# One store of a cross-covariance attention kernel, half of it sent in parts of 92, 4 and 32 partitions

## The chip, the core and the metric

The kernel runs on one core of one Trainium2 chip. The metric is device time in microseconds (us): the median of the runs of the program. Beside it there is one profiled execution with its trace. The work of the core is done by TensorE (PE, with its weight loads shown as PEld), VectorE (DVE), ScalarE (ACT) and GpSimd (POOL); SyncE (SP) issues nearly all transfers between the chip's memory (HBM) and the on-chip buffers, and sixteen DMA engines carry them out.

## The reference, cut to what matters

```python
batch, heads, seq, dim = 8, 12, 512, 64          # Q, K, V: float32
Q_norm = Q / (np.linalg.norm(Q, axis=-2, keepdims=True) + 1e-10)
K_norm = K / (np.linalg.norm(K, axis=-2, keepdims=True) + 1e-10)
attn = np.einsum('bhnd,bhne->bhde', Q_norm, K_norm)
attn = softmax(attn, axis=-1)                    # written out with max, exp and sum
out  = np.einsum('bhnd,bhde->bhne', V, attn)
```

There are 96 heads. For each, a 64x64 matrix is made of Q and K, normalised, put through a softmax, and applied to V. Three inputs of 12.58 MB are read and one output of 12.58 MB is written.

## The kernel before, in words

**Tiling.** Four heads make a unit `u` (24 of them), two units a step `s` (`S` = 12), two steps a pair `w` (6). Q and K of a unit are loaded (`load_qk`, lines 182 to 186), cast to bf16 (`cast_qk`, L206), multiplied into Gram matrices (`grams`, L226), from which the norms and the logits come; V is loaded (`load_v`), cast, transposed (`vtrans`) and copied to `vt`. The output matmuls (`outs`, L312) write PSUM, and `ocopy` (L165 on ACT, L167 on DVE) brings the results into a tile `so[s, i]` of 128 partitions.

**Stores.** `so[s, i]` with `i` 0 or 1 holds half of a step: 128 partitions, for each of two units `r` a contiguous run of 2 KB (`J * D` = 512 floats). So a store moves 256 rows of 2 KB, 512 KB in all. `store(s, i)` issues it as one DMA on SP (L200); the very last tile (`s` = 11, `i` = 1) goes in two DMAs of 256 KB with rows of 1 KB. There are 25 store DMAs. Every DMA of the kernel spans 128 partitions.

**Order.** All work is put into one list by a planner (`Order.run`) that simulates the engines and a DMA queue of eight; each transfer has a due rank. It puts 5 of the stores between the loads, and the last 20 DMAs on SP are all stores, in the order of `s` and `i`. On SP a DMA waits for its data and, by one of eight semaphores used in turn, for the complete landing of the DMA issued eight places earlier on SP. The end of the kernel (L492) waits for all of them.

Of the kernel before, what the change touches and what calls it, by code (L numbers as in the profile page):

```python
# [102 lines left out]
def kernel(  # L103
# [7 lines left out]
    nc = tc.nc  # L111
# [3 lines left out]
    S = U // 2  # L115
# [3 lines left out]
    ONE = 3  # L119
    HELD, UNTIL = ("lk", 1, 1), ("cq", 0, 1)  # L120
    BOTH = S - 8

# [36 lines left out]
    qk32, v32, vb, qkb, gram, scr, kq, n2, r8, kqs, rq, lg, ex, ab, vps, vt, po, so = ({} for _ in range(18))  # L161
# [35 lines left out]
    def store(s, i, k=None):  # L197
        rows = slice(None) if k is None else slice(k * (J // 2), (k + 1) * (J // 2))
        o = Of[s // 2, s % 2, i].rearrange("p r (j d) -> p r j d", d=D)
        nc.sync.dma_start(out=o[:, :, rows], in_=so[s, i][:, :, rows])  # L200

    def cast_qk(u, x):
# [138 lines left out]
    for i in range(NB["ab"]):  # L341
        a = const.tile([128, HU, 2 * D], BF16, name=f"ab{i}")
# [17 lines left out]
    def piece(key, engines, after, behind, rank, fn, *args):  # L360
        if key[0] in ("cv", "vc", "oc", "kq", "sc"):
            plan.add(key, engines, after, behind, rank, lambda eng: fn(eng, *args))
        else:
            plan.add(key, engines, after, behind, rank, lambda eng: fn(*args))

    def back(kind, i, n, *rest):
        return (kind, i - n, *rest) if i - n >= 0 else None
# [17 lines left out]
    for u in range(U):  # L385
        s, r = divmod(u, 2)
# [21 lines left out]
    for w in range(W):  # L408
        both = 2 * w >= BOTH
        for r in range(2):  # L410
# [24 lines left out]
    for s in range(S):  # L435
        for x in range(4):
            i, k = divmod(x, 2)
            n = 4 * s + x - 2
            wait = [("oc", n // 4, n % 4)] if n >= 0 else []
            order = [("ou", s, x - 1) if x else back("ou", s, 1, 3)]  # L440
            piece(("ou", s, x), {"PE": 0.5}, [("vc", s // 2, *t) for t in turns(s // 2) if t[0] // 2 == k] + [("nm", s)] + wait, order, R["ou"] + 0.01 * s, outs, s, x)
            n = 2 * s + i - NB["so"]
            free = [("st", n // 2, n % 2)] if k == 0 and n >= 0 else []
            order = [("oc", s, x - 1) if x else back("oc", s, 1, 3)]
            piece(("oc", s, x), {"ACT": 0.6, "DVE": (0.68, BIAS["oc"])} if s >= BOTH else {"ACT": 0.6}, [("ou", s, x)] + free, order, R["oc"] + 0.01 * s, ocopy, s, x)
        for i in range(2):
            order = [("st", s, 0) if i else back("st", s, 1, 1)]
            if (s, i) == (S - 1, 1):

                piece(("sh", s, i), {"DMA": 0.67}, [("oc", s, 2)], order, v_at(2 * s + i) + ST_LAG, store, s, i, 0)  # L450
                piece(("st", s, i), {"DMA": 0.67}, [("oc", s, 3)], [("sh", s, i)], v_at(2 * s + i) + ST_LAG, store, s, i, 1)
            else:
                piece(("st", s, i), {"DMA": X}, [("oc", s, 2 * i), ("oc", s, 2 * i + 1)], order, v_at(2 * s + i) + ST_LAG, store, s, i)
# [43 lines left out]
```

## Time and profile before

| what | us |
|---|---|
| median of 3 runs | 128.83 (128.76 to 129.06) |
| profiled execution, its own time | 129.06 |
| its span, first to last instruction | 127.3 |
| last compute instruction ends (ACT, L165) | 115.34 |
| last store DMA issued on SP | 117.29 |
| DVE busy / PE busy / ACT busy | 93.0 / 79.4 / 72.5 |
| mean rate of the DMA engines | 398 GB/s |

The page shows one execution. Its second part cuts the span into 40 slices of 3.18 us; the row DMA is the mean busy share of the 16 DMA engines. Part 3 lists the DMA queues: q1 is SP's, q10 ACT's, and the two of kind "instruction" fetch program code. A DMA that is split over all engines is finished when each of the sixteen has finished its share; the trace marks each of these sixteen landings, without the number of the engine.

### The profile page before, as it was taken

The page shows a single profiled execution, that of the slowest core. Times are in us where ns is not written, and L with a number is a line of the kernel's source. Part 1 is how long each engine was busy: PE and PEld are TensorE (multiplying, and loading weights), DVE is VectorE, ACT ScalarE, POOL GpSimd, SP SyncE. Part 2 cuts the span into 40 slices and gives each one's busy share as a digit, 9 for nine tenths or more (in the row PEclk, how much of TensorE's full clock was granted, in tenths as well). Part 3 has the DMA queues.
Part 4 walks back from the last instruction along what each step waited for, and adds up shares of the span by engine and source line. Part 5 has one row for each costly group of instructions (what it writes and reads, how often), then busy time and mean ns, then how long its engine had stood idle before and what let it go on. Part 6 is the DMA issues. An engine that isn't in the chain of part 4 may idle for free.

```text
span 127.3 us, 4884 instructions
## 1 busy us (share of the span) xinstructions
PE 79.4 (62%) x2128; PEld 64.0 (50%) x2128; DVE 93.0 (73%) x141; ACT 72.5 (57%) x220; POOL 36.3 (28%) x40
## 2 busy tenths in 40 slices
PE   0065384894844589859873996698975869580000
PEld 0055372773633568648661885486764748460000
DVE  3263649959999899998986798999999799820000
ACT  4000441569777068785792789384949969972000
POOL 4005306300915913033064203213453361200000
PEclk9999999999997556995999589655699995955555
DMA  3999999999999999999999999999999999999992
GB/s 107 404 434 409 430 409 418 415 440 402 425 429 416 407 418 424 407 416 422 430 415 409 417 424 417 417 420 424 406 413 407 406 401 406 400 407 407 408 352 98
DMA packets 15605, 50.64 MB, mean 398 GB/s; under 512 B 1120, under 2 KB 1632, under 8 KB 14176
## 3 DMA queue, kind: packets, MB, share of 16 engines
q1 hardware_dynamic: 15296, 49.29, 96.2%
q10 hardware_dynamic: 288, 1.05, 2.1%
q8 instruction: 16, 0.26, 0.7%
q14 instruction: 5, 0.04, 0.1%
HBM read 37.75 MB, written 12.58 MB: 396 GB/s over the span
## 4 chain that ended last, share of the span: by engine, by line
DVE 31%; DMA 20%; PE 18%; ACT 14%; issue 4%; SPq 2%; POOL 1%; DVEq 0%; POOLq 0%; ACTq 0%
DMA qk<-in_K_dram 14%; PE gram L226 12%; DVE qkb L206 11%; DVE scr L233 6%; DMA qk<-in_Q_dram 5%; DVE ab L284 5%; ACT so L165 4%; ACT vt L165 4%; ACT ex L275 4%; PE vps L295 3%; DVE vt L167 3%; DVE n L245 3%; PE po L312 2%; ACT kq L165 1%; SPq L184 1%
## 5 line engine op out<-in xcount | busy, mean ns | idle before, releaser
L226 PE MATMUL gram<-qkb 32*128 32x128 bf16 (+1 forms) x1504 | 35.6, 255 | 21.9 <-DVE qkb L206 8.8
L206 DVE CAST qkb<-qk 128x1024 bf16<-128x1024 f32 x48 | 37.3, 801 | 8.5 <-DMA qk<-in_Q_dram 7.0
L226 PEld LDWEIGHTS <-qkb 32*128 32x128 bf16 (+1 forms) x1504 | 29.8, 114 | 26.8 <-DVE qkb L206 11.6
L169 POOL TENSOR_SCALAR vb<-v 128x1024 bf16<-128x1024 f32 x19 | 21.2, 1126 | 45.1 <-DMA v<-in_V_dram 45.0
L165 ACT COPY so<-po 128x512 f32<-128x512 f32 x45 | 25.0, 593 | 6.6 <-PE po L312 6.4
L165 ACT COPY vt<-vps 128x1024 bf16<-128x1024 bf16 (+1 forms) x18 | 17.8, 987 | 15.9 <-PE vps L295 15.9
L312 PE MATMUL po<-ab,vt 128*64 128x128 bf16 x384 | 21.1, 259 | 6.0 <-issue 2.4
L295 PE MATMUL vps<-identb,vb 128*128 128x128 bf16 x192 | 19.3, 255 | 5.1 <-POOL vb L169 3.1
L256 POOL TENSOR_TENSOR kqs<-kq,r 64x512 f32<-64x512 f32 x12 | 13.7, 1143 | 26.9 <-ACT r L252 13.7
L312 PEld LDWEIGHTS <-vt 128*64 128x64 bf16 x384 | 15.3, 131 | 10.3 <-issue 5.4
L233 DVE SCALAR_TENSOR_TENSOR scr<-gram,eye 64x512 f32<-64x512 f32 x24 | 16.5, 688 | 4.7 <-PE gram L226 4.4
L295 PEld LDWEIGHTS <-vb 128*128 128x128 bf16 x192 | 14.1, 113 | 9.0 <-POOL vb L169 4.5
L275 ACT ACTIVATE ex<-lg,rq 128x64 f32<-128x64 f32 x48 | 14.5, 321 | 2.8 <-PE lg L269 2.8
L165 ACT COPY kq<-gram 64x512 f32<-64x512 f32 x12 | 7.0, 580 | 13.6 <-DVE scr L233 13.4
L284 DVE TENSOR_TENSOR ab<-ex,rinv 64x256 bf16<-64x256 f32 x24 | 13.2, 548 | 0.6
L275 ACT ACTIVATION_READ_ACCUMULATOR ex<-lg,rq 128x1 f32 x48 | 10.2, 213 | 0.0
L167 DVE CAST vb<-v 128x1024 bf16<-128x1024 f32 x5 | 7.4, 1483 | 1.3 <-DMA v<-in_V_dram 1.2
L269 PE MATMUL lg<-eye,kqs 64*128 64x64 f32 x48 | 6.9, 274 | 2.3 <-POOL kqs L256 1.8
L245 DVE TENSOR_REDUCE n<-scr 128x8 f32<-128x512 f32 x12 | 8.2, 679 | 0.1
L167 DVE COPY vt<-vps 128x1024 bf16<-128x1024 bf16 (+1 forms) x8 | 7.9, 1019 | 0.1
L269 PEld LDWEIGHTS lg<-eye,kqs 64*128 64x128 f32 x48 | 4.8, 168 | 4.3 <-POOL kqs L256 2.5
L281 DVE RECIPROCAL rinv<-esum 128x4 f32<-128x4 f32 x12 | 2.1, 172 | 2.6 <-ACT ex L275 2.5
(17 smaller groups left out, 16.0 us busy)
## 6 DMA issues: line engine op xcount, KB each, us to landing
out_dram<-so SPq DMA_DIRECT2D x23, 512.0 KB, 10.2
v<-in_V_dram SPq DMA_DIRECT2D x11, 1024.0 KB, 17.2
qk<-in_Q_dram SPq DMA_DIRECT2D x8, 1024.0 KB, 17.5
qk<-in_K_dram SPq DMA_DIRECT2D x8, 1024.0 KB, 18.5
qk<-in_Q_dram SPq DMA_DIRECT2D x8, 512.0 KB, 12.2
qk<-in_K_dram SPq DMA_DIRECT2D x6, 512.0 KB, 12.4
qk<-in_K_dram ACTq DMA_DIRECT2D x2, 512.0 KB, 6.3
v<-in_V_dram SPq DMA_DIRECT2D x2, 512.0 KB, 10.6
```

Of the source, the lines that this page charges most:

```text
L165: nc.scalar.copy(o, i)
L167: nc.vector.tensor_copy(o, i)
L169: nc.gpsimd.tensor_scalar(out=o, in0=i, scalar1=1.0, scalar2=0.0, op0=ALU.mult, op1=ALU.add)
L206: nc.vector.tensor_copy(qkb[u][:, :, x * D:(x + 1) * D], qk32[s][:, x, r])
L226: nc.tensor.matmul(gram[s][:, h, r, 0], x, x, start=(t == 0), stop=(t == (T if u < WIDE else J) - 1))
L233: nc.vector.scalar_tensor_tensor(out=scr[s][half], in0=gram[s][half, :, :, 0, half].rearrange("p h r d -> p (h r) d"), scalar=1e-20, in1=e ...
L245: nc.vector.tensor_reduce(out=n2[s], in_=scr[s], axis=mybir.AxisListType.X, op=ALU.add)
L256: (nc.vector if eng == "DVE" else nc.gpsimd).tensor_tensor(out=kqs[s][HI], in0=kq[s][HI], in1=r8[s][HI, :, None].to_broadcast([D, 2 * HU, ...
L275: nc.scalar.activation(e[:, h, :], lg[s][:, h, :], AF.Exp, scale=rq[s][:, h:h + 1], accum_out=z[:, h:h + 1])
L284: nc.vector.tensor_tensor(out=a[half, :, half], in0=e[half], in1=ri[half, :, None].to_broadcast([D, HU, D]), op=ALU.mult,)
L295: nc.tensor.transpose(ps[:, c, n, :], vb[w][:, J * c + j].rearrange("p r d -> p (r d)"), identb)
L312: nc.tensor.matmul(po[s, x][e * D:(e + 1) * D, j].rearrange("p r d -> p (r d)"), v, ab[s][:, h, :])
```

## The change

The store of step `S - 3` = 9, `i` = 1 (the sixth DMA from the end of SP's list of 20) is sent as four DMAs in place of one. Its half `r` = 1 goes as one DMA of 128 partitions. Its half `r` = 0 goes as three: partitions 0 to 91, 92 to 95 and 96 to 127. As the change is described, the first two of these run on the four lowest DMA engines alone, and the third on all sixteen.

```diff
+    FEW = (S - 3, 1)
...
     def store(s, i, k=None):
         rows = slice(None) if k is None else slice(k * (J // 2), (k + 1) * (J // 2))
         o = Of[s // 2, s % 2, i].rearrange("p r (j d) -> p r j d", d=D)
+        if (s, i) == FEW:
+            for a, b in ((0, 92), (92, 96), (96, 128)):
+                nc.sync.dma_start(out=o[a:b, 0], in_=so[s, i][a:b, 0])
+            nc.sync.dma_start(out=o[:, 1], in_=so[s, i][:, 1])
+            return
         nc.sync.dma_start(out=o[:, :, rows], in_=so[s, i][:, :, rows])
```

The order of all other instructions on every engine stays as it was.

## The prediction

> **What bounds the kernel now.** I began with the page's slices and queues.
>
> ```profile
> span 127.3 us, 4884 instructions
> DMA  3999999999999999999999999999999999999992
> ## 3 DMA queue, kind: packets, MB, share of 16 engines
> q1 hardware_dynamic: 15296, 49.29, 96.2%
> q10 hardware_dynamic: 288, 1.05, 2.1%
> q8 instruction: 16, 0.26, 0.7%
> q14 instruction: 5, 0.04, 0.1%
> ```
>
> From the second slice to the last but one the DMA engines are full. No compute engine is: DVE is busy for 73% of the span. So the kernel is bound by bytes, and the chain of waits, which follows only compute instructions, ends 12 us before the span does. The end is made by the stores. I looked at SP's last rows next: the timeline's last row, then the time to landing of the stores from 93 us on, then SP's waits from 85 us on.
>
> ```profile
> 117.29 0.71 SPq L200 DMA_DIRECT2D out_dram<-so  x1
> ```
>
> ```profile
> DMA to landing us min/median/max: 9.0/10.2/10.2
> ```
>
> ```profile
> SPq L200 <- DMA out_dram<-so: 8.8, 14, 1.0
> SPq L492 <- DMA out_dram<-so: 8.2, 3, 6.9
> ```
>
> The last store is issued at 117.29 and lands 9.0 us later, at 126.29; SP's closing wait (L492) is for it, and the span ends 0.97 us after. The profiled execution took 129.06 us, 1.8 more than its span and 0.23 above the median of the runs, 128.83. I make the sum against the landing at 126.29 and take 0.23 off at the end.
>
> The question is whether all sixteen engines finish together. Narrow windows answer it (second last column: busy share of 16 engines; last: GB/s).
>
> ```profile
> 121.00:122.00 1.00, 0.00 (x0) 0.00 (x0) 0.00 (x0) 0.00 (x0) 0.00 (x0) 0.50 1.05 402
> 122.50:123.00 0.50, 0.00 (x0) 0.00 (x0) 0.00 (x0) 0.00 (x0) 0.00 (x0) 0.50 0.96 358
> 123.00:123.50 0.50, 0.00 (x0) 0.00 (x0) 0.00 (x0) 0.00 (x0) 0.00 (x0) 0.50 0.80 299
> 123.50:124.00 0.50, 0.00 (x0) 0.00 (x0) 0.00 (x0) 0.00 (x0) 0.00 (x0) 0.50 0.68 260
> 124.00:124.50 0.50, 0.00 (x0) 0.00 (x0) 0.00 (x0) 0.00 (x0) 0.00 (x0) 0.50 0.55 205
> 125.00:125.50 0.50, 0.00 (x0) 0.00 (x0) 0.00 (x0) 0.00 (x0) 0.00 (x0) 0.50 0.55 195
> 125.50:126.00 0.50, 0.00 (x0) 0.00 (x0) 0.00 (x0) 0.00 (x0) 0.00 (x0) 0.50 0.22 74
> ```
>
> They don't. Full is 1.05; from 124 to 125.5 the share is 0.55, so some eight engines work on while eight are done. The sixteen landing marks of the last store in the trace say the same: 123.10, 123.13, 123.20, 123.50, 123.68, 123.96, 124.37, 124.60, and then eight from 125.87 to 126.29. Every transfer of this kernel gives each engine the same bytes, so the lag comes from elsewhere. Queue q8 has 16 packets of 16 KB; the trace puts each at 0.88 to 0.96 us, on one engine alone. Followed from landing to landing, all engines step evenly, except that after each q8 packet one engine falls back by about 1.4 us; eight engines do so, twice each. The 8 KB packets of q14 (0.31 us) fall on the other eight, with steps of 0.5 to 0.8. So the program's own code is fetched unevenly over the DMA engines, and that sets who ends last.
>
> **The change, part by part.**
>
> *Price of a row.* At 402 GB/s an engine moves 25.1 GB/s, 0.082 us for a row of 2 KB; stores land 1.28 us apart with 16 rows per engine, 0.080 each. I take 0.080.
>
> *Rows moved.* The half `r` = 0 gave each engine 8 rows. By the change's own account it now gives the four lowest 92/4 + 4/4 + 32/16 = 26 rows and the other twelve 2. So +18 rows = +1.44 us for four engines, -6 rows = -0.48 us for twelve.
>
> *Three more DMAs.* Each adds one completion mark per engine (a 4-byte packet, 9 ns in the trace). The four get three more, the twelve one more: +0.03 and +0.01 us. On SP each issue took 0.37 to 0.85 us in this stretch, which lies within the 1.28 us between two stores.
>
> [...]
>
> *SP's queue.* Each SP DMA waits for the one eight places earlier. Three more DMAs push the five stores behind them three places down, so each is issued some 3 x 1.28 = 3.84 us later: the last at about 120 us. The early engines need its rows only from about 123.8 and the late ones from 125, so 3.8 us and more hide it (before, the first packet moved 1.0 us after the first issue). The last DMA now also waits for the part of 92 partitions. On four early engines that is done at about 118.5 (their landing of the DMA before, 116.6 to 117.0, plus 23 rows = 1.84), which is earlier. Cost nothing; with the cover gone it would be up to 3.84.
>
> *Where the rows go.* All hangs on which engines are the lowest four, and the trace does not number them. If they are among the eight that carry no q8 packet, they end at 123.10 to 124.60 plus 1.47, that is 124.57 to 126.07, and the eight late ones at 126.29 - 0.47 = 125.82. Unless the slowest of that early half (124.60) is one of the four, or the next (124.37, which then ends at 125.84, as good as level), the late eight set the end at 125.82: a gain of 0.47. With the slowest, the end is 126.07: a gain of 0.22. I take 0.47, since the four marks nearest together, 123.10 to 123.50, are the likeliest to be neighbours, and keep 0.22 for the range.
>
> *Reading from other partitions.* No row shows a store that gives one engine 23 rows in place of 8. [...] I take nothing, by the nearest rows: packets of 2, 4 and 8 KB took 84, 159 and 309 ns on loads and stores alike, whatever the other fifteen engines were reading or writing at the time. [...]
>
> **Sum.** Profiled: the last landing moves from 126.29 to 125.82, and with what lies around the span unchanged 129.06 - 0.47 = 128.59. The median of the runs lies 0.23 lower: 128.36. I say 128.4.
>
> **The rivals.**
>
> *The four lowest fetch code (slower).* If even one of the four is among the eight late engines, that one ends at 125.87 to 126.29 plus 1.47, so 127.3 to 127.8, and nothing takes work off it. Price +1.05 to +1.47: about 130.2. The point from which it decides is a landing before of 126.29 - 1.47 = 124.82 or later; between 124.60 and 125.87 there is no engine, so it is one or the other. For it: only 8 of 16 engines are early, and all four must be. When the very first load begins, the sixteen first packets come in four groups of four by their durations; in the two groups that I could follow, two engines later fetch code and two do not. Were these groups neighbours by number, the lowest four would hold two late ones. Against: engines that serve one fetch queue in a fixed rotation of eight look like one half of sixteen, not like picks among them, and then it is a matter of which half.
>
> *The early four fill up (no change).* One of them is the engine of 124.60, or their rows run somewhat slower than 0.080: with 18 rows at 0.09 to 0.10 the slowest early engine ends at 126.2 to 126.4. Time 128.6 to 128.95.
>
> *The split isn't what it says.* If 92 partitions also run on all sixteen engines, nothing is moved; three completion marks cost 0.03: 128.85. Against it: nothing in the trace, as all its DMAs span 128 partitions. [...]
>
> **How the numbers follow.** About 0.2% (0.26 us) is what a measurement of this kernel can tell from no change. The early engines take the rows, gain 0.47: 0.42. One of the four was late: 0.38. Filled up: 0.16, and no split: 0.04, together the 0.20 for no change. The likeliest case alone has 128.2 to 128.6 (a row at 0.082 and the lowest run at one end, half a gain at the other). The two signs lie so close in chance that the range must hold the slow case too: up to 130.4, its 130.3 with the spread of the runs.
>
> **What would show it.** Right: the busy share falls from 1.05 later than 122.5 and from there to nothing within some 2 us; the last store's eight last marks come 0.47 earlier; four marks in the middle come 1.47 later; SP issues its last store near 120. Wrong: a share of 0.25 (four engines) or less for 1.5 us at the end, with twelve marks earlier and at least one beyond 127.3; or a last store that is issued after 121 and lands only then; or rows of 2 KB that take over 84 ns while the part of 92 is under way.

## The result, and the profile after

The changed kernel takes 128.61 us (median of 20 runs, 128.46 to 128.80) against 128.93 for the kernel before on the same chip (20 runs, 128.76 to 129.10). The ratio is 0.9976, with a 95% interval of 0.997 to 0.9983: a gain of 0.31 us, between 0.22 and 0.39. The profiled execution took 128.80 us, 0.26 less than that of before. In every profiled execution of this document the time is that of the last landing mark plus 2.62 to 2.79 us: the last mark decides.

The page of the changed kernel, slices and queues: the bytes and the code packets are as before, q1 has 24 packets more.

```profile
span 127.0 us, 4887 instructions
DMA  4999999999999999999999999999999999999993
q1 hardware_dynamic: 15320, 49.29, 96.4%
q8 instruction: 16, 0.26, 0.7%
```

Of the 24, one completion mark more on each of twelve engines and three more on each of four would be 12 + 12: that is the count if the parts of 92 and 4 partitions run on four engines alone. The timeline of SP at the end shows the parts (L204, L205) and the last five stores behind them:

```profile
110.63 2.80 SPq L204 DMA_DIRECT2D out_dram<-so  x3
114.40 0.37 SPq L205 DMA_DIRECT2D out_dram<-so  x1
115.75 4.76 SPq L207 DMA_DIRECT2D out_dram<-so  x5
```

The last issue starts at 120.05, 2.76 later than before, and no engine waited for it: the last store's marks follow those of the store before it by some 0.68 us, as they did before the change. Narrow windows of the changed kernel (second last column: share of the 16 DMA engines):

```profile
122.50:123.00 0.50, 0.00 (x0) 0.00 (x0) 0.00 (x0) 0.00 (x0) 0.00 (x0) 0.50 0.87 336
123.00:123.50 0.50, 0.00 (x0) 0.00 (x0) 0.00 (x0) 0.00 (x0) 0.00 (x0) 0.50 0.87 334
123.50:124.00 0.50, 0.00 (x0) 0.00 (x0) 0.00 (x0) 0.00 (x0) 0.00 (x0) 0.50 0.78 281
124.00:124.50 0.50, 0.00 (x0) 0.00 (x0) 0.00 (x0) 0.00 (x0) 0.00 (x0) 0.50 0.81 287
124.50:125.00 0.50, 0.00 (x0) 0.00 (x0) 0.00 (x0) 0.00 (x0) 0.00 (x0) 0.50 0.65 229
125.00:125.50 0.50, 0.00 (x0) 0.00 (x0) 0.00 (x0) 0.00 (x0) 0.00 (x0) 0.50 0.12 41
125.50:126.00 0.50, 0.00 (x0) 0.00 (x0) 0.00 (x0) 0.00 (x0) 0.00 (x0) 0.50 0.03 10
```

Where before 0.55 of the engines were at work from 124 to 125.5, now some twelve are (0.81) until 124.5, and the fall comes half a microsecond earlier. One engine is left over: 0.03 after 125.5. The landing marks of the last store say which: four early ones (122.48, 122.69, 123.03, 124.00), eleven between 124.81 and 125.54, and a single one at 126.05. The marks of the part of 92 partitions belong to four engines: 118.70, 118.95, 119.30, 119.94. Each of these four ends 6.11 or 6.12 us later (124.81, 125.07, 125.41, 126.05), so the slowest of them stays the last to the end.

The two profiles alone don't show the gain. In the one of the changed kernel the store before the parts already stood 0.27 us earlier (last mark 119.52 against 119.79), and from there to the end it took 6.53 us against 6.50: nothing was won in this execution. The gain of 0.31 us is that of the 20 runs; the repeat below has a profile in which the change wins its full share.

### The profile page after: what moved, and what is told of

It is laid out like the page before. It is cut to its first block, busy times and chain, and to the rows that moved or that the text cites. A ratio compares the mean times of both kernels' runs of the same rounds, so it can differ in the third digit from the quotient of the medians.

```text
span 127.0 us, 4887 instructions
## 1 busy us (share of the span) xinstructions
PE 77.7 (61%) x2128; PEld 62.9 (50%) x2128; DVE 92.8 (73%) x141; ACT 72.5 (57%) x220; POOL 36.6 (29%) x40
## 3 DMA queue, kind: packets, MB, share of 16 engines
q1 hardware_dynamic: 15320, 49.29, 96.4%
## 4 chain that ended last, share of the span: by engine, by line
DVE 39%; DMA 21%; PE 13%; ACT 11%; issue 4%; POOL 2%; DVEq 0%; SPq 0%; POOLq 0%; ACTq 0%
DMA qk<-in_Q_dram 21%; DVE qkb L213 15%; PE gram L233 9%; DVE scr L240 7%; DVE ab L291 6%; ACT vt L166 4%; DVE vb L168 4%; ACT ex L282 3%; ACT so L166 3%; PE vps L302 3%; DVE n L252 2%; DVE vt L168 2%; DVE so L168 2%; PE po L319 1%; ACT kq L166 1%
## 5 line engine op out<-in xcount | busy, mean ns | idle before, releaser
L213 DVE CAST qkb<-qk 128x1024 bf16<-128x1024 f32 x48 | 36.4, 780 | 8.5 <-DMA qk<-in_Q_dram 6.9
L302 PE MATMUL vps<-identb,vb 128*128 128x128 bf16 x192 | 20.2, 262 | 5.8 <-POOL vb L170 3.7
L319 PE MATMUL po<-ab,vt 128*64 128x128 bf16 x384 | 19.3, 242 | 5.2 <-issue 2.7
L302 PEld LDWEIGHTS <-vb 128*128 128x128 bf16 x192 | 14.7, 117 | 10.0 <-POOL vb L170 5.1
L319 PEld LDWEIGHTS <-vt 128*64 128x64 bf16 x384 | 13.8, 121 | 9.2 <-issue 4.6
L291 DVE TENSOR_TENSOR ab<-ex,rinv 64x256 bf16<-64x256 f32 x24 | 13.9, 579 | 0.6
L282 ACT ACTIVATION_READ_ACCUMULATOR ex<-lg,rq 128x1 f32 x48 | 10.2, 213 | 0.0
L276 PE MATMUL lg<-eye,kqs 64*128 64x64 f32 x48 | 6.4, 259 | 2.6 <-issue 1.5
## 6 DMA issues: line engine op xcount, KB each, us to landing
out_dram<-so SPq DMA_DIRECT2D x22, 512.0 KB, 10.2
```

Of the source, the lines that this page charges most:

```text
L213: nc.vector.tensor_copy(qkb[u][:, :, x * D:(x + 1) * D], qk32[s][:, x, r])
L276: nc.tensor.transpose(l[:, h, :], kqs[s][HI, 2 * h:2 * h + 2].rearrange("p r d -> p (r d)"), eye2[HI])
L282: nc.scalar.activation(e[:, h, :], lg[s][:, h, :], AF.Exp, scale=rq[s][:, h:h + 1], accum_out=z[:, h:h + 1])
L291: nc.vector.tensor_tensor(out=a[half, :, half], in0=e[half], in1=ri[half, :, None].to_broadcast([D, HU, D]), op=ALU.mult,)
L302: nc.tensor.transpose(ps[:, c, n, :], vb[w][:, J * c + j].rearrange("p r d -> p (r d)"), identb)
L319: nc.tensor.matmul(po[s, x][e * D:(e + 1) * D, j].rearrange("p r d -> p (r d)"), v, ab[s][:, h, :])
```

## The experiments

Each time stands against runs of the kernel before on the same chip; those runs had medians of 128.93 to 129.02. "Rows" are runs of 2 KB; the line changed is the `for` of the change, if nothing else is shown.

**Splitting without shifting.**

```diff
-            for a, b in ((0, 92), (92, 96), (96, 128)):
+            for a, b in ((0, 96), (96, 112), (112, 128)):
```

> The same store in the same number of DMAs, but with parts of 96, 16 and 16 partitions, which give every engine 8 rows as before: split without shift. Theory (rows moved off the late engines make the gain): no change against before, within 0.2%, near 128.9; the sixteen marks of the last store spread over 3.2 us as before. Rival (the gain comes from the splitting itself, from smaller parts or from the later issue of the stores behind): as fast as the changed kernel, 0.3 us under before.

Measured: 129.03 against 128.99, ratio 1.0002 (0.9993 to 1.0011). The last store's marks run from 123.04 to 126.33, as wide as before. From the last mark of the store before the parts to the end it is 6.50 us, as before. So three DMAs more, and the later issue behind them, cost nothing and bring nothing that can be told: the gain is in the shift.

**The whole half on four engines.**

```diff
-            for a, b in ((0, 92), (92, 96), (96, 128)):
+            for a, b in ((0, 124), (124, 128)):
```

> Parts of 124 and 4 partitions: the whole half on the four lowest engines, 32 rows each in place of 8 (+24), the other twelve -8. Theory (the changed kernel now ends on the slowest of the four lowest, at 126.05): six rows more on it, 126.05 + 0.48 = 126.5 for the last mark, the late eight at 125.4; 0.48 slower than the changed kernel, 0.1 to 0.2 us slower than before. Rival (the late eight still set the end in most runs): 0.16 faster than the changed kernel, 0.5 faster than before.

Measured: 128.96, ratio 1.0003 (0.9994 to 1.0011): the gain is gone, though the slow-down of 0.1 to 0.2 that I expected is not resolved. The trace's last mark is at 126.52, as reckoned, and the one before it at 125.85. Its windows show a long thin tail that the changed kernel has not:

```profile
125.00:125.50 0.50, 0.00 (x0) 0.00 (x0) 0.00 (x0) 0.00 (x0) 0.00 (x0) 0.50 0.16 55
125.50:126.00 0.50, 0.00 (x0) 0.00 (x0) 0.00 (x0) 0.00 (x0) 0.00 (x0) 0.50 0.07 25
126.00:126.50 0.50, 0.00 (x0) 0.00 (x0) 0.00 (x0) 0.00 (x0) 0.00 (x0) 0.50 0.02 8
```

One engine (0.02 to 0.07 of sixteen) sets the end: more rows for the four is worse from here on.

**Numbering the engines.**

```diff
-            for a, b in ((0, 92), (92, 96), (96, 128)):
+            for a, b in ((0, 96), (96, 108), (108, 116), (116, 120),
+                         (120, 123), (123, 125), (125, 126), (126, 128)):
```

> One look to number the engines: the half leaves in parts of 96, 12, 8, 4, 3, 2, 1 and 2 partitions, so that the part of n partitions marks only its engines. Theory (the eight engines that fetch no PE code are the lowest eight): the part of 8 has eight early marks and none from the late eight, the part of 12 has four late ones. Rival (they are picked from among the sixteen): the part of 8 has late marks too, beyond the four lowest. Either way the parts of 4, 3, 2 and 1 tell which of the four lowest is the one that ends last. Its time is not read: eight small DMAs in a row take most of SP's eight places.

The part of 96 has sixteen marks, eight from 116.97 to 118.92 and eight from 119.65 to 120.11. The part of 12 has seven early and five late ones, that of 8 six early (117.38 to 119.29) and two late (120.11, 120.21), that of 4 only early ones: 117.70, 118.02, 118.39, 118.98. So none of engines 0 to 3 is late, two of 4 to 7, three of 8 to 11 and three of 12 to 15: the rival is right that they are picked. (The trace gives no numbers. That a part on n engines uses 0 to n - 1 is my assumption, in line with the account of the change; no run shows it, and every number of an engine in this document rests on it.) The slowest of the four lowest is in the parts of 3, 2 and 1 (119.17, 119.34, 119.50), so it is engine 0, 1.5 us behind the earliest engine, which by that assumption no part can leave out. The part of 96 has sixteen marks, and each smaller part as many as it has partitions: with the sixteen of the other half 64 in place of the 16 of one store, and q1 has 48 packets more than before (15344 against 15296). In the changed kernel the part of 92 has four marks. These counts leave out one mark more that the parts on fewer than sixteen engines have; in the changed kernel it comes 0.46 us after the issue of the part of 92 and 0.43 us after that of the part of 4 (111.09 and 112.25), long before their data. The one run took 130.18 us.

**Less code to fetch.** From the kernel before:

```diff
-        for t in range(T if u < WIDE else J):
+        for t in range(4):
...
-                nc.tensor.matmul(gram[s][:, h, r, 0], x, x, start=(t == 0), stop=(t == (T if u < WIDE else J) - 1))
+                nc.tensor.matmul(gram[s][:, h, r, 0], x, x, start=(t == 0), stop=(t == 3))
```

> The kernel before with Gram matrices over 4 of the 16 (or 8) rows, so that TensorE has about 2250 instructions fewer and its code takes 7 packets of 16 KB in place of 16; the transfers are the same, the Gram sums are partial. Theory (PE's code packets make the lag of the late engines): seven engines late by 1.4 us once, none twice; the last store's marks spread over about 1.5 us in place of 3.2 and the time falls by some 1.4 us to 127.5. Rival (those engines are late for another reason, or the end hangs on compute): spread of 3.2 us and no change beyond 0.3 us.

Measured: 127.63 against 128.99, ratio 0.99 (0.9885 to 0.9914), 1.3 us faster, and the repeat (below) 127.54, ratio 0.9894. The page of the repeat shows the same transfers, half the code packets (8; I had reckoned 7) and still full DMA engines:

```profile
span 126.0 us, 2644 instructions
DMA  4999999999999999999999999999999999999993
q1 hardware_dynamic: 15296, 49.29, 97.1%
q8 instruction: 8, 0.13, 0.4%
```

The marks of the last store run from 123.03 to 125.21 in the first trace and from 123.26 to 125.05 in the repeat: a spread of 2.2 and 1.8 us (expected 1.5) in place of 3.2. The earliest mark is about where it was (123.10 before), so it is the late engines that gain, and less computing as such has not made all transfers faster. The 0.13 MB of code left out, spread over all engines at 402 GB/s, would be an estimated 0.33 us.

**The change where half of the lag is gone.** The edit of the last experiment and the change together, beside the former alone.

> The change on top of the shortened Gram matrices (4 of 16 rows, partial sums), where half of TensorE's code packets are gone. Theory (the change pays only because code fetching holds eight engines back): without most of that lag the four lowest end 1.47 later than in the shortened kernel, at about 125.7 to 126.0 against its last mark of 125.21, so it is 0.4 to 0.8 us slower than the shortened kernel. Rival (the parts pay by themselves): 0.3 us faster than the shortened kernel.

> The shortened Gram matrices without the change once more, beside e9 on the same chip: 1.3 us (1.1 to 1.5) faster than before by every theory.

Measured: 128.53 with the change (ratio to before 0.9969, 0.9958 to 0.998), 127.54 without it (0.9894, 0.988 to 0.9908): the same edit that gains 0.3 us now costs 1.0, a little more than expected (0.8 between the two profiles). The windows of the shortened kernel with the change:

```profile
124.00:124.50 0.50, 0.00 (x0) 0.00 (x0) 0.00 (x0) 0.00 (x0) 0.00 (x0) 0.50 0.26 92
124.50:125.00 0.50, 0.00 (x0) 0.00 (x0) 0.00 (x0) 0.00 (x0) 0.00 (x0) 0.50 0.16 55
125.00:125.50 0.50, 0.00 (x0) 0.00 (x0) 0.00 (x0) 0.00 (x0) 0.00 (x0) 0.50 0.09 31
```

A share of 0.26 is four engines, 0.09 a little over one. Four marks stand alone, 124.77, 125.04, 125.47 and 125.84; the other twelve are done by 124.39. Without the change the DMA engines of this kernel are done earlier:

```profile
124.00:124.50 0.50, 0.00 (x0) 0.00 (x0) 0.00 (x0) 0.00 (x0) 0.00 (x0) 0.50 0.53 186
124.50:125.00 0.50, 0.00 (x0) 0.00 (x0) 0.00 (x0) 0.00 (x0) 0.00 (x0) 0.50 0.07 23
```

This settles the cause: the change pays only because of the lag that code fetching makes.

**The changed kernel once more, with fewer rows, and earlier.** The repeat has no edit. Then

```diff
-            for a, b in ((0, 92), (92, 96), (96, 128)):
+            for a, b in ((0, 76), (76, 80), (80, 128)):
```

and, with the parts of the change,

```diff
-    FEW = (S - 3, 1)
+    FEW = (S - 6, 1)
```

> The changed kernel once more, beside the next three on the same chip: 0.3 us (0.2 to 0.4) faster than before by every theory; its last mark belongs to the slowest of the four lowest engines, some 0.5 us after the late eight.

> Parts of 76, 4 and 48 partitions: the four lowest get 23 rows in place of 26 (+15 over before), the others 3 in place of 2 (-5). Theory (the slowest of the four, engine 0, ends the changed kernel 0.5 us after the late eight): engine 0 ends at 126.05 - 0.24 = 125.81, the late eight at 125.54 + 0.08 = 125.62, so 0.24 faster than the changed kernel and 0.5 faster than before. Rival (in most runs the late eight end last, as the prediction had it): 0.08 slower than the changed kernel, 0.24 faster than before.

> The change's parts of 92, 4 and 32 put on a store three steps earlier (S - 6). Theory (rows are moved between engines that are always full, and SP's queue hides the later issue wherever it is): same as the changed kernel within 0.1 us. Rival (the gain needs the shift at the very end, or the queue's shorter backlog costs something there): no gain over before, or a loss.

Measured, against 129.02: the repeat 128.71 (ratio 0.9973, 0.9963 to 0.9982), fewer rows 128.52 (0.9963, 0.9951 to 0.9976), earlier 128.53 (0.9966, 0.9953 to 0.9978). The rival of "earlier" falls: the place of the shift doesn't matter by more than can be told. Fewer rows gain 0.48 against 0.35 for the repeat; the intervals overlap, so that they beat the change is likely and not shown. The traces tell why the step is smaller than 0.24: in the repeat the slowest mark of the four lowest came 0.21 earlier than in the first profile (119.91 against 120.12 after the part of 4), and the last five marks of its last store lie together from 125.66 to 125.93. From the last mark of the store before the parts to the end the repeat took 6.02 us (119.90 to 125.93) against 6.53 in the first profile and 6.50 before, and the kernel with fewer rows took 6.10 (119.80 to 125.91). Engine 0's lag changes from one execution to the next, for a reason that no run shows; so does which group ends last, and my "some 0.5 us after the late eight" held in one profile of two.

**The eight lowest engines.**

```diff
-            for a, b in ((0, 92), (92, 96), (96, 128)):
-                nc.sync.dma_start(out=o[a:b, 0], in_=so[s, i][a:b, 0])
-            nc.sync.dma_start(out=o[:, 1], in_=so[s, i][:, 1])
+            for a, b in ((0, 96), (96, 104), (104, 112), (112, 120), (120, 128)):
+                nc.sync.dma_start(out=o[a:b], in_=so[s, i][a:b])
```

> The same store as a part of 96 partitions and four of 8 partitions, both halves in each: the eight lowest engines get 20 rows in place of 16 (+4), the other eight 12 (-4). By the stairs two of the late engines are among engines 4 to 7. Theory: these two end 4 rows later, 126.29 + 0.32 + 0.03 = 126.6, so 0.35 us slower than before: what the change would have cost had its engines been late ones, at a quarter of its rows. Rival (the numbering read from the stairs is wrong, and the lowest eight are all early): 0.3 faster than before.

Measured: 128.98, ratio 0.9996 (0.9987 to 1.0005), no change. Both expectations missed. My error can be read in the stairs: the two late engines among 4 to 7 are not the latest of the eight. Going back from their marks at 120.11 and 120.21 by two parts of one row each, they stand at about 119.7 and 119.8 in the part of 96, where the latest is at 120.11. With 0.3 to 0.4 in hand, 0.35 more brings them level with the old end, while the other late ones gain. The trace of this run agrees. Its parts of 8 again have six early marks and two late ones, and these two were the earliest of the late eight in the store before (119.19 and 119.29, the latest 119.82), with 0.5 to 0.6 in hand. After the last part of 8 they stand at 120.98 and 121.08, behind the other late ones (at most 120.78 after the part of 96), and they are the last from then on, to 126.15 against 126.29 before.

**Both small gains together.** Parts of 76, 4 and 48 on the store of `S - 6`.

> Parts of 76, 4 and 48 partitions on the store three steps earlier: the two experiments that came out ahead of the changed kernel together. Theory: the late eight set the end with 5 rows less, 126.29 - 0.40 + 0.01 = 125.9, so 0.4 faster than before and at most 0.1 from either of the two alone. Rival (position and size add up): 0.6 faster than before.

Measured: 128.49 against 128.93, ratio 0.9965 (0.9952 to 0.9977), 0.45 faster; last mark 125.76. That is nearest to the theory's 0.4, but the interval is a gain of 0.30 to 0.62 us, and the rival's 0.6 lies just inside it: that position and size don't add up is likely and not shown.

## Why the prediction was right, point by point

**The range** says little: 128.2 to 130.4 held the slow rival and no change as well. The point was 128.4, and the likeliest case alone had 128.2 to 128.6, at whose edge 128.61 lies. What counts is what follows.

**The direction and the mechanism** held. DMA engines that lag by their code packets set the end (halving the packets: -1.3 us), the shift takes rows off them, and the split itself is free (ratio 1.0002).

**The price of a row** held. In the changed kernel the four engines land the part of 92 partitions 1.85 us after the store before (116.85 to 118.70, 117.10 to 118.95): 23 rows at 0.080. The late eight need 6.02 us from the last mark of the store before the parts to their own last mark (119.52 to 125.54), against 6.50 before (119.79 to 126.29): -0.48, where the sum had -0.47. The four themselves need 7.96 us (118.09 to 126.05 for the slowest), against 6.51 of an early engine before (116.59 to 123.10): +1.45, where the sum had +1.47. Reading 92 partitions by four engines cost nothing, as those 23 rows at 0.080 show, and I was right to take nothing.

**The three extra DMAs and SP's queue** were free, as taken: splitting alone gave a ratio of 1.0002. In the profile of before a store took 10.2 us from issue to landing while one landed each 1.28 us, so some eight were under way at once. Of SP's waits from 85 us on, the closing one shows where its time went:

```profile
SPq L499 <- DMA out_dram<-so: 5.4, 3, 3.9
```

The closing wait is 3.9 us at the longest in place of 6.9, since the last store is issued later, at 120.05 as reckoned, though 2.76 and not 3.84 later than before. The last store waited for the part of 92 partitions, whose slowest engine landed at 119.94, only 0.42 after the store before the parts (119.52) and not a full 1.28. So that part did set the last issue. The prediction had put it at about 118.5 on all four engines; it was 118.70 to 119.94. The prediction also took 123.8 as the time from which the early engines need the last store's rows. That overlooked the four early engines that get fewer rows: the first of them had finished the store before at 121.80. The issue at 120.05 was early enough for it too.

**What was mis-sized is the end of the slowest of the four.** The forecast took 0.47, arguing that the four marks nearest together (123.10 to 123.50) are the likeliest neighbours. They are not: before their part the four lowest stood 0.41, 0.66, 1.00 and 1.65 behind the earliest engine (116.85, 117.10, 117.44 and 118.09 against 116.44). Only a slowest engine that stands at least 1.94 us (1.47 + 0.47) before the last of the late eight leaves the full 0.47. In the first profile engine 0 stood 1.43 before it (118.09 against 119.52), too little for any gain, and 6.53 us against 6.50 is none. In the repeat it stood some 2.0 before it (119.73 less 23 rows, against 119.90), and the gain is 0.48. The median gain of 0.31 lies between, and engine 0's lag differs between executions; with two profiles only, 0.31 as a mixture of such cases is likely and not shown. Neither 0.47 nor the 0.22 kept for the range allows for it. "One of the four was late" at 0.38 was a fair chance for what I knew. The argument against it, that a fixed rotation of eight looks like one half of sixteen, was wrong, as the late engines are, by the numbering of the third experiment, spread over 4 to 15. That none of the lowest four is late was therefore partly luck; numbering the engines, as in the third experiment, was needed to know.

**The slow rival's mechanism** is real under its own condition: where the four lowest are not early by the rows that they get, they set the end (+1.0 us in the shortened kernel).

## What to carry to other kernels

When a kernel is bound by bytes, look past the mean share at how the sixteen engines end: a slope in the last few windows is time that a shift of rows can win, here 0.3 to 0.5 us of 129. Here the shift won only where the engines that received it were early: 0.3 us with 16 code packets, and a loss of 1.0 us with 8. So find out which they are (here parts of 1, 2, 3, 4 and 8 partitions left as many marks) before sizing it, and size it for the slowest of them. It has to be sized again when the program's length changes: with half the code packets the marks of the last store spread over 1.8 and 2.2 us in place of 3.2.

## What the runs showed of the hardware that I had not expected

With 2240 TensorE instructions fewer (2644 instructions in place of 4884, nothing else left out) queue q8 has 8 packets of 16 KB in place of 16, so these carry TensorE's code. Each is on one DMA engine, for 0.88 to 0.99 us in the profiles of the kernel before and of the changed one, and in the landings of the kernel before it sets that engine back by some 1.4 us (why by more than it lasts is open). Eight engines take them, twice each in the kernel before. In the one run that numbered all engines these are, by the numbering assumed there, none of engines 0 to 3, two of 4 to 7, three of 8 to 11 and three of 12 to 15. Eight packets fewer made this byte-bound kernel 1.3 us faster (127.63 against 128.99, repeated at 127.54 against 128.93) with not one byte of data less (q1 49.29 MB in both).
